# A decoder trunk on one core: both activation parts against one weight load, halves added at the eviction

## The chip, the cores and the metric

The kernel runs on one core of one Trainium2 chip. The metric is the device time of one execution in microseconds (us). Three runs of the kernel before are shown; beside them stands one profiled execution, from which every duration below is read.

## The reference

Two layers act on 256 tokens of 1024 features, in float32. Each layer is a token mixer (differential attention, block attention and latent attention side by side, merged by gates) and then a squared-ReLU MLP, each with a norm ahead and a norm behind. What matters here:

```python
h = _rms_norm(x, norm_mix_pre[l])
proj = einsum('bsd,de->bse', h, w_in[l])          # holds dq, dk, dv, mq, mk, mv, latents, gates
... three attentions, gates, output projection, x = x + norm(...)
h = _rms_norm(x, norm_mlp_pre[l])
u = square(relu(einsum('bsd,df->bsf', h, w_up[l])))      # 1024 -> 4096
x = x + _rms_norm(einsum('bsf,fd->bsd', u, w_down[l]), norm_mlp_post[l])
```

## The kernel before

**Arithmetic.** Every float32 operand of a projection is split into a high and a low part of a narrower type (fp32r), and a product is the sum of three matmuls: high weights by high activations, high by low, low by high (`mm3`, lines 174 to 179). `mm_group` (line 181) runs that triple over the eight 128-row tiles of the 1024 features, so that a block of 128 output features by 256 tokens is 24 matmuls of 256 columns, accumulated in PSUM.

**Weights.** `chunk` (line 132) loads 512 KB on the SP queue into one of five raw buffers, ScalarE (ACT) copies it to the high part (line 129), VectorE (DVE) subtracts to get the low part (line 130). There are six buffers of each part. `load_f` (line 167) brings a weight slab of 256 output columns as two chunks of four row tiles each; both of its 128-column blocks use both chunks, so a chunk comes free when the second block has passed it.

**Projections concerned.** The query and key projections of the differential attention (`dqk`) and of the block attention (`mqk`) go through `qk_proj` (line 441): four slabs each and layer, two blocks to a slab. Both blocks of a slab write the two halves of one PSUM tile of 512 columns, and one DVE instruction (line 448) evicts it, times the tokens' 1/rms. The up projection (`up`, line 721) does the same for seven of its eight groups and two slabs a group; its eviction is a ReLU on ACT (line 748), a square on ACT into the high part of `u` (line 751), a square on GpSimd (POOL, line 752) and a subtraction on DVE for the low part (line 753). The group 0 of the up projection, the value projections, the gates and the rest take other paths.

**Order of the work.** The MLP runs `up(g)` and then `down(g - 1)` for each group. In the mixer, dv and dqk are projected first, then in the program come the bias and rope constants (line 470), the latents' transposes (line 473), the differential attention, the projections mv and mqk, the block attention, the latent attention and the gates. The order in which each engine's queue holds these is worked out at build time by a planner (line 837): it places instructions by their place in the program and by when its own clock says that their inputs and buffers are there. On the chip each engine then follows that order.

**Buffers that the change touches.** PSUM tiles of the projections come from `mm_tile` (line 74), a pool of two banks. Small SBUF tiles come from `prep_tile` (line 68), a pool of three buffers that serves many names, among them `cn` (two tiles of latents, line 419, read by the transposes of line 458), `oh` (the one-hot load of the attention bias, line 261), `cb`, `lamv` and `r`.

Of the kernel before, what the change touches and what calls it, by code (L numbers as in the profile page):

```python
# [29 lines left out]
            2.7524476990947733e-06, -2.3874981991411914e-08)  # L30
# First relative distance of each T5 bucket that distances 0..255 can reach.
BUCKET_START = tuple(range(17)) + (21, 27, 35, 46, 59, 77, 99, 128, 166, 216)
# [3 lines left out]
def trunk(ctx: ExitStack, tc: tile.TileContext, x, positions, rel_bias, norm_mix_pre, norm_mix_post,  # L36
# [45 lines left out]

# [1 line left out]
    # Rows of vectors that act on features once those lie on partitions.  # L84
    n_rows = 16 + 16 + 4 + 2 + 2
# [37 lines left out]

# [1 line left out]
    def split(dst_hi, dst_lo, src, quick=False):  # L125
# [6 lines left out]
    def chunk(src, nk, c, name, parts=None, spare=None, quick=False):  # L132
        """One load of weights and its two parts; `spare` is a pool that is idle now."""
        n = nk * c
        raw = raws.tile([128, 1024], F32, tag="raw", name=f"raw_{name}")
        rv = raw[:, :n].rearrange("p (k c) -> p k c", k=nk)
        nc.sync.dma_start(rv, src)
        if spare is None:
            hi = whi.tile([128, 1024], F32R, tag="hi", name=f"hi_{name}")
            lo = wlo.tile([128, 1024], F32R, tag="lo", name=f"lo_{name}")  # L140
        else:
            pool, tag = spare
            hi = pool.tile([128, 1024], F32R, tag=tag, name=f"hi_{name}")
            lo = pool.tile([128, 1024], F32R, tag=tag, name=f"lo_{name}")
        if parts is None:
            split(hi[:, :n], lo[:, :n], raw[:, :n], quick)
        else:
            at = 0
            for v in parts(raw):
                m = v.shape[1] * v.shape[2]  # L150
                o = [t[:, at:at + m].rearrange("p (a b) -> p a b", a=v.shape[1]) for t in (hi, lo)]
                split(o[0], o[1], v)
                at += m
        return [(hi[:, k * c:(k + 1) * c], lo[:, k * c:(k + 1) * c]) for k in range(nk)]
# [4 lines left out]
    def load_t(w2d, c0, c, name, kts=KT):  # L159
        """Weights that move: kts tiles of [128, c]."""  # L160
        nk = 1024 // c
        r = []
        for k0 in range(0, kts, nk):
            r += chunk(wslice(w2d, k0, nk, c0, c), nk, c, f"{name}_{k0}")
        return r

    def load_f(w2d, c0, name, kts=KT):
        """Weights that stay: two blocks of 128 columns, kts tiles each."""
        r = []
        for k0 in range(0, kts, 4):  # L170
            r += chunk(wslice(w2d, k0, 4, c0, 256), 4, 256, f"{name}_{k0}")
        return [[(h[:, b * 128:(b + 1) * 128], l[:, b * 128:(b + 1) * 128]) for h, l in r] for b in range(2)]
# [8 lines left out]
    def mm_group(ps, stats, movs):  # L181
        n = len(stats)
        for i in range(n):
            mm3(ps, stats[i], movs[i], i == 0, i == n - 1)

    def toks(act, t):
        return [(h[:, t * 128:(t + 1) * 128], l[:, t * 128:(t + 1) * 128]) for h, l in act]

# [1 line left out]
    def new_act(name):  # L190
        return [slab_r(f"{name}{p}") for p in range(4)]

    def act_views(tiles):
        return [(tiles[k // 2][:, 0, k % 2, :], tiles[k // 2][:, 1, k % 2, :]) for k in range(KT)]

# [35 lines left out]
    def post_norm(xt, ps2, wpost, eps_col):  # L231
        """x += rms_norm(ps2) * wpost"""
        parts = small_tile("pnp", 2)
        yw = slab_tile([128, D], "yw")
        def weigh(h):
            nc.vector.tensor_tensor(yw[:, h * 512:(h + 1) * 512], ps2[h][:],
                                    wpost[:, h * 512:(h + 1) * 512], op=OP.mult)
        for h in range(2):
            nc.scalar.activation(junk, ps2[h][:], AF.Square, scale=1.0 / 32.0, accum_out=parts[:, h:h + 1])
            if h == 0:  # L240
                weigh(0)
        v = small_tile("pnv", 1)
        nc.vector.tensor_scalar(v, parts[:, 0:1], parts[:, 1:2], EPS if eps_col is None else eps_col,
                                op0=OP.add, op1=OP.add)
        q = small_tile("pnq", 1)
        rpow(q, v, 1)
        weigh(1)
        for h in range(2):
            s = slice(h * 512, (h + 1) * 512)
            nc.vector.scalar_tensor_tensor(xt[:, s], yw[:, s], q[:, 0:1], xt[:, s],  # L250
                                           op0=OP.mult, op1=OP.add)

# [1 line left out]
    bias = consts.tile([128, 9, 256], F32, name="bias")  # L254
# [22 lines left out]
    def setup_rope():  # L277
# [11 lines left out]
        for t in range(2):  # L289
            for j in range(2):  # L290
                V.tensor_scalar(ang[:, t, j, :], fr, pf[:, t:t + 1], None, op0=OP.mult)
        # Index 0: sine.  Index 1: cosine, the sine a quarter turn on.
        V.tensor_scalar(k[:, :, 0, :], ang[:, :, 0, :], 1.0 / math.pi, MAGIC, op0=OP.mult, op1=OP.add)
# [23 lines left out]
    def setup_lam():  # L317
# [10 lines left out]
        for l in range(DEPTH):  # L328
            li = 0.8 - 0.6 * math.exp(-0.3 * l)
            nc.vector.tensor_scalar(lam[:, l:l + 1], dots[:, 2 * l:2 * l + 1], dots[:, 2 * l + 1:2 * l + 2], li,  # L330
                                    op0=OP.subtract, op1=OP.add)
            # The weights come out of the chip negated: the sign goes here.
            nc.vector.tensor_scalar(subc[:, l:l + 1], cols[:, 38 + l:39 + l], -(1.0 - li), None, op0=OP.mult)

# [1 line left out]
    last_exp = [None]  # L336
# [35 lines left out]
    def av_f(ps, pt, v0, v1):  # L372
        """ps [c, 256 queries] = v^T p^T"""
        nc.tensor.matmul(ps, v0, pt[:, 0:256], start=True, stop=False)
        nc.tensor.matmul(ps[:, 128:256], v1, pt[:, 256:384], start=False, stop=True)

# [1 line left out]
    def load_c(l, k1, n):  # L378
# [5 lines left out]
    def mixer(l, xs, tiles, wc, before):  # L384
# [6 lines left out]

        # latent queries, keys and the shared rope key, token-major
        wc = wc or load_c(l, 0, 4)
# [30 lines left out]

        # 1/rms of every token along the free axis, on all partitions
        prb = tr_tile("prb")
# [14 lines left out]
        def qk_proj(off_q, off_k, p, scale, name):  # L441
            r = slab_tile([128, 2, 2, 256], f"{name}{p}")
            for j, off in ((0, off_q), (1, off_k)):
                w = load_f(win, off + p * 256, f"{name}{l}{p}{j}")
                ps = mm_tile(f"p{name}")
                for b in range(2):
                    mm_group(ps[:, b * 256:(b + 1) * 256], w[b], act)
                nc.vector.scalar_tensor_tensor(r[:, j], ps.rearrange("p (b s) -> p b s", b=2),
                                               scale if j == 0 else 1.0, rb2, op0=OP.mult, op1=OP.mult)
            return r  # L450

        # transposed latents
        def latents():
# [20 lines left out]

        # differential attention
        o_a = []
# [44 lines left out]

        # block attention: one block holds the whole sequence, so each query sees its own block
        mv = v_proj(OFF['mv'], "mv")
# [14 lines left out]

        # latent attention
        uq = []  # L540
# [85 lines left out]

        # gates and the products of the three branches, two feature blocks at a time
        branches = [[(o[j // 2][:, 0, j % 2, :], o[j // 2][:, 1, j % 2, :]) for j in range(4)] for o in (o_a, o_b, o_c)]
# [32 lines left out]

        # output projection
        wpost = load_post(norm_mix_post, l, sig_after)
# [14 lines left out]
    def finish(accs, held, xs, wpost, eps_cols, nxt, wcol, stored=None):  # L678
        """The last rows of a projection, the first half of the tokens ahead, and the norm that follows."""
        for t in range(2):  # L680
# [14 lines left out]
    def out_proj(l, w2d, act, wpost, xs):  # L695
        """x += rms_norm(mixed @ w_out); the next block's input follows each half of the tokens."""
        tiles = new_act("h2")
# [14 lines left out]
    def mlp(l, xs, tiles, before):  # L712
# [8 lines left out]
        def up(g):  # L721
# [20 lines left out]
            for p in range(2):  # L742
                w = load_f(wu, g * 512 + p * 256, f"up{l}{g}{p}")
                ps = mm_tile("pu")
                for j in range(2):
                    mm_group(ps[:, j * 256:(j + 1) * 256], w[j], act)
                r = prep_tile("r")
                nc.scalar.activation(r, ps[:], AF.Relu)
                rv = r.rearrange("p (b s) -> p b s", b=2)
                hi, lo = us[g][p][:, 0], us[g][p][:, 1]  # L750
                nc.scalar.activation(hi, rv, AF.Square)  # L751
                nc.gpsimd.tensor_tensor(r, r, r, op=OP.mult)  # L752
                nc.vector.tensor_tensor(lo, rv, hi.bitcast(F32), op=OP.subtract)
# [87 lines left out]
```

## Time and profile before

| what | value |
|---|---|
| runs, median (lowest to highest) | 875.62 us (873.63 to 876.04) |
| profiled execution, first to last instruction | 874.3 us |
| instructions | 14960, of these 5820 matmuls and as many weight loads |
| share of the span busy: TensorE (PE), DVE, ACT, POOL | 98%, 62%, 54%, 12% |
| DMA | 154.27 MB, mean 176 GB/s |
| TensorE's granted clock, mean | 0.997 of 2.4 GHz |

The page gives no time of the profiled execution but its span; the median of the runs stands 1.3 us above that. A matmul's listed duration overlaps with its neighbours' (a group of 256-column matmuls shows 283 ns each), so what a matmul costs in a full stream is read from the distance of the starts, not from the duration.

### The profile page before, as it was taken

What the parts mean: (1) busy time and instruction counts of PE and PEld (TensorE: products, weight loads), DVE (VectorE), ACT (ScalarE), POOL (GpSimd) and SP (SyncE); (2) the same over time, 40 slices, a digit from 0 to 9 for tenths busy, and PEclk for the clock granted to TensorE, in tenths of its full rate; (3) what the DMA queues carried; (4) which work ended last, traced back from release to release, by engine and by line L of the source; (5) the groups of instructions that cost most, each with busy time, mean ns of one, the idle gap of its engine ahead of it and who ended that gap; (6) DMA issues with size and microseconds to landing.
All of it is one profiled execution on the core that took longest, in us unless ns stands there. A gap on an engine that the chain in (4) does not pass through costs nothing.

```text
span 874.3 us, 14960 instructions
## 1 busy us (share of the span) xinstructions
PE 858.1 (98%) x5820; PEld 791.0 (90%) x5820; DVE 539.6 (62%) x921; ACT 468.9 (54%) x820; POOL 107.1 (12%) x130
## 2 busy tenths in 40 slices
PE   7999999999999999999999999999999999999997
PEld 6988999899988999999899899999998899999995
DVE  6757688457867445446575768954578754554452
ACT  6536675644546444445464757664544664444441
POOL 2211210001311000000100012000033010000010
PEclk9999999999999999999999999999999999999999
DMA  8865544356666656667738553546558466665631
GB/s 275 260 168 180 144 124 134 107 178 184 203 232 195 185 182 189 191 193 212 228 97 248 146 149 97 150 117 189 177 187 270 145 218 191 192 193 182 186 115 49
DMA packets 109798, 154.27 MB, mean 176 GB/s; under 512 B 5103, under 2 KB 89136, under 8 KB 109728
## 3 DMA queue, kind: packets, MB, share of 16 engines
q1 hardware_dynamic: 108448, 149.70, 56.4%
q10 hardware_dynamic: 608, 2.11, 0.7%
q0 software_dynamic: 672, 1.51, 0.6%
q8 instruction: 46, 0.75, 0.4%
q14 instruction: 24, 0.20, 0.1%
HBM read 151.19 MB, written 2.11 MB: 175 GB/s over the span
## 4 chain that ended last, share of the span: by engine, by line
PE 88%; issue 4%; DMA 3%; DVE 2%; ACT 1%; POOL 1%; SPq 0%; POOLq 0%; DVEq 0%; ACTq 0%
PE pu L176 7%; PE pu L178 7%; PE pu L177 7%; PE pd L177 6%; PE pd L178 6%; PE pd L176 6%; PE pg L176 5%; PE pg L177 5%; PE pg L178 5%; PE pb L178 3%; PE pb L177 3%; PE pb L176 3%; PE pmqk L178 2%; PE pmqk L177 2%; PE pmqk L176 2%
## 5 line engine op out<-in xcount | busy, mean ns | idle before, releaser
L177 PE MATMUL pu<-h,hi_up 128*128 128x256 f32 x448 | 126.9, 283 | 0.0
L178 PE MATMUL pu<-h,lo_up 128*128 128x256 f32 x448 | 126.8, 283 | 0.0
L176 PE MATMUL pu<-h,hi_up 128*128 128x256 f32 x448 | 126.7, 283 | 0.0
L130 DVE TENSOR_TENSOR lo_wd<-raw_wd,hi_wd 128x1024 fp32r<-128x1024 f32 x64 | 77.7, 1225 | 74.5 <-ACT hi_wd L129 74.5
L129 ACT ACTIVATE hi_wd<-raw_wd 128x1024 fp32r<-128x1024 f32 x64 | 67.0, 1058 | 82.6 <-PE pu L177 38.0
L176 PE MATMUL pg<-h,hi_g 128*128 128x256 f32 x384 | 110.6, 288 | 0.4 <-ACT lqk L602 0.4
L178 PE MATMUL pg<-h,lo_g 128*128 128x256 f32 x384 | 109.7, 286 | 0.0
L177 PE MATMUL pg<-h,hi_g 128*128 128x256 f32 x384 | 109.1, 284 | 0.0
L130 DVE TENSOR_TENSOR lo_up<-raw_up,hi_up 128x1024 fp32r<-128x1024 f32 x64 | 80.2, 1258 | 38.8 <-ACT hi_up L129 38.5
L129 ACT ACTIVATE hi_up<-raw_up 128x1024 fp32r<-128x1024 f32 x64 | 67.9, 1064 | 59.5 <-PE pu L177 29.0
L176 PE MATMUL pd<-hi_wd,u 128*128 128x512 f32 x256 | 99.9, 390 | 0.0
L177 PE MATMUL pd<-lo_wd,u 128*128 128x512 f32 x256 | 99.8, 390 | 0.0
L178 PE MATMUL pd<-hi_wd,u 128*128 128x512 f32 x256 | 99.6, 389 | 0.0
L176 PEld LDWEIGHTS pu<-h,hi_up 128*128 128x128 f32 x448 | 85.9, 192 | 0.6
L177 PEld LDWEIGHTS pu<-h,hi_up 128*128 128x128 f32 x448 | 85.9, 192 | 0.5
L178 PEld LDWEIGHTS pu<-h,lo_up 128*128 128x128 f32 x448 | 85.9, 192 | 0.1
L130 DVE TENSOR_TENSOR lo_g<-raw_g,hi_g 128x1024 fp32r<-128x1024 f32 x48 | 58.6, 1222 | 39.0 <-ACT hi_g L129 38.7
L176 PEld LDWEIGHTS pg<-h,hi_g 128*128 128x128 f32 x384 | 73.5, 191 | 1.4 <-ACT lqk L602 0.6
L177 PEld LDWEIGHTS pg<-h,hi_g 128*128 128x128 f32 x384 | 73.5, 191 | 0.5 <-issue 0.3
L178 PEld LDWEIGHTS pg<-h,lo_g 128*128 128x128 f32 x384 | 73.5, 191 | 0.1
L129 ACT ACTIVATE hi_g<-raw_g 128x1024 fp32r<-128x1024 f32 x48 | 50.5, 1057 | 40.2 <-PE pg L177 32.2
L752 POOL TENSOR_TENSOR r<-r 128x512 f32<-128x512 f32 x28 | 30.6, 1094 | 262.1 <-ACT u L751 230.9
(293 smaller groups left out, 2109.2 us busy)
## 6 DMA issues: line engine op xcount, KB each, us to landing
raw_up<-in_w_up_dram SPq DMA_DIRECT2D x64, 512.0 KB, 3.9
raw_wd<-in_w_down_dram SPq DMA_DIRECT2D x64, 512.0 KB, 4.2
raw_g<-in_w_in_dram SPq DMA_DIRECT2D x48, 512.0 KB, 3.8
raw_br<-in_w_branch_dram SPq DMA_DIRECT2D x24, 512.0 KB, 4.1
raw_dqk<-in_w_in_dram SPq DMA_DIRECT2D x16, 512.0 KB, 5.2
raw_mqk<-in_w_in_dram SPq DMA_DIRECT2D x16, 512.0 KB, 4.1
raw_wo<-in_w_out_dram SPq DMA_DIRECT2D x16, 512.0 KB, 3.9
raw_dv<-in_w_in_dram SPq DMA_DIRECT2D x8, 512.0 KB, 4.9
```

The source lines that it names most:

```text
L129: nc.scalar.activation(dst_hi, src, AF.Copy)
L130: nc.vector.tensor_tensor(dst_lo, src, dst_hi.bitcast(F32), op=OP.subtract)
L176: i = nc.tensor.matmul(ps, sh, mh, start=first, stop=False)
L177: nc.tensor.matmul(ps, sh, ml, start=False, stop=False)
L178: nc.tensor.matmul(ps, sl, mh, start=False, stop=last)
L752: nc.gpsimd.tensor_tensor(r, r, r, op=OP.mult)
```

## The change

`mm_wide` takes the place of `mm_group` in `qk_proj` and in `up` for the groups 1 to 7. The high and the low part of the activations, which lie in one tile, are passed in one matmul of 512 columns against the high weights: the high part goes to the first 256 columns of a PSUM bank, the low part to the second. The low weights by the high activations are accumulated on the first 256 columns. A block of 128 features so takes a whole PSUM tile, and `add_wide` evicts it: ACT copies the second half to SBUF, DVE adds the first half to it. In `qk_proj` the sum goes to a new tile `sum` of the prep pool, and the multiplication by 1/rms reads that. In `up` the ReLU and the square become one DVE instruction in place, ACT copies the result to the high part, and POOL's square is gone. The comment lines that the diff removes as well are left out here.

```diff
     def mm_group(ps, stats, movs):
         n = len(stats)
         for i in range(n):
-            mm3(ps, stats[i], movs[i], i == 0, i == n - 1)
+            mm3(ps, stats[i][:2], movs[i][:2], i == 0, i == n - 1)
+
+    def mm_wide(ps, stats, movs):
+        n = len(stats)
+        main = ps[:, 0:256]
+        for i in range(n):
+            (sh, sl), (mh, _, mhl) = stats[i], movs[i]
+            nc.tensor.matmul(ps.rearrange("p (b s) -> p b s", b=2), sh, mhl, start=i == 0, stop=False)
+            nc.tensor.matmul(main, sl, mh, start=False, stop=i == n - 1)
+
+    def add_wide(o, ps):
+        nc.scalar.activation(o, ps[:, 256:512], AF.Copy)
+        nc.vector.tensor_tensor(o, ps[:, 0:256], o, op=OP.add)
...
+    def both(tile, b):
+        return tile[:, 0, b, :], tile[:, 1, b, :], tile[:, :, b, :]
...
     def act_views(tiles):
-        return [(tiles[k // 2][:, 0, k % 2, :], tiles[k // 2][:, 1, k % 2, :]) for k in range(KT)]
+        return [both(tiles[k // 2], k % 2) for k in range(KT)]
...
                 w = load_f(win, off + p * 256, f"{name}{l}{p}{j}")
-                ps = mm_tile(f"p{name}")
+                s = prep_tile("sum")
                 for b in range(2):
-                    mm_group(ps[:, b * 256:(b + 1) * 256], w[b], act)
-                nc.vector.scalar_tensor_tensor(r[:, j], ps.rearrange("p (b s) -> p b s", b=2),
+                    ps = mm_tile(f"p{name}")
+                    mm_wide(ps, w[b], act)
+                    add_wide(s[:, b * 256:(b + 1) * 256], ps)
+                nc.vector.scalar_tensor_tensor(r[:, j], s.rearrange("p (b s) -> p b s", b=2),
...
                 w = load_f(wu, g * 512 + p * 256, f"up{l}{g}{p}")
-                ps = mm_tile("pu")
+                r = prep_tile("r")
                 for j in range(2):
-                    mm_group(ps[:, j * 256:(j + 1) * 256], w[j], act)
-                r = prep_tile("r")
-                nc.scalar.activation(r, ps[:], AF.Relu)
+                    ps = mm_tile("pu")
+                    mm_wide(ps, w[j], act)
+                    add_wide(r[:, j * 256:(j + 1) * 256], ps)
+                nc.vector.scalar_tensor_tensor(r, r, 0.0, r, op0=OP.max, op1=OP.mult)
                 rv = r.rearrange("p (b s) -> p b s", b=2)
                 hi, lo = us[g][p][:, 0], us[g][p][:, 1]
-                nc.scalar.activation(hi, rv, AF.Square)
-                nc.gpsimd.tensor_tensor(r, r, r, op=OP.mult)
+                nc.scalar.activation(hi, rv, AF.Copy)
                 nc.vector.tensor_tensor(lo, rv, hi.bitcast(F32), op=OP.subtract)
```

## Rows read from the trace of the kernel before

**Rows 1.** The page: busy us, share of the span, instructions of each engine.
```profile
PE 858.1 (98%) x5820; PEld 791.0 (90%) x5820; DVE 539.6 (62%) x921; ACT 468.9 (54%) x820; POOL 107.1 (12%) x130
```

**Rows 2.** The page: the chain that ended last, share of the span by engine.
```profile
PE 88%; issue 4%; DMA 3%; DVE 2%; ACT 1%; POOL 1%; SPq 0%; POOLq 0%; DVEq 0%; ACTq 0%
```

**Rows 3.** Groups by line and shape: line, engine, names, shapes, count, busy, mean, idle before.
```profile
L177 PE MATMUL pu<-h,hi_up 128*128 128x256 f32 x448 | 126.9, 283 | 0.0
L177 PE MATMUL pmqk<-h,hi_mqk 128*128 128x256 f32 x128 | 37.6, 294 | 0.0
L177 PE MATMUL pdqk<-h,hi_dqk 128*128 128x256 f32 x128 | 36.2, 283 | 0.0
```

**Rows 4.** Timeline of PE: start us, us, what. One stream of each width, first and last.
```profile
296.53 0.28 PE L176 MATMUL pu<-h,hi_up 128*128 128x256 f32 x1
...
302.29 0.28 PE L176 MATMUL pu<-h,hi_up 128*128 128x256 f32 x1
...
399.79 0.39 PE L176 MATMUL pd<-hi_wd,u 128*128 128x512 f32 x1
...
408.41 0.39 PE L178 MATMUL pd<-hi_wd,u 128*128 128x512 f32 x1
```

**Rows 5.** Groups by line and shape: evictions and elementwise steps, before or nearest to the new ones.
```profile
L752 POOL TENSOR_TENSOR r<-r 128x512 f32<-128x512 f32 x28 | 30.6, 1094 | 262.1 <-ACT u L751 230.9 <-DVE lo_wd L130 31.2
L751 ACT ACTIVATE u<-r 128x512 fp32r<-128x512 f32 x28 | 17.7, 632 | 0.8
L748 ACT ACTIVATE r<-pu 128x512 f32<-128x512 f32 x28 | 16.2, 579 | 2.5 <-PE pu L178 2.5
L250 DVE SCALAR_TENSOR_TENSOR x<-yw,pnq,x 128x512 f32<-128x512 f32 x16 | 11.3, 749 | 0.4
L448 DVE SCALAR_TENSOR_TENSOR dqk<-pdqk,rb 128x512 f32<-128x512 f32 x8 | 5.5, 684 | 0.0
L670 DVE TENSOR_TENSOR ob<-sc,ob 128x256 fp32r<-128x256 f32 x8 | 3.3, 418 | 0.1
L669 ACT ACTIVATE ob<-sc 128x256 fp32r<-128x256 f32 x8 | 3.1, 383 | 2.5 <-PE sc L375 2.4
```

**Rows 6.** Timeline of ACT and DVE behind the block boundary at 302.29.
```profile
302.37 1.06 ACT L129 ACTIVATE hi_wd<-raw_wd 128x1024 fp32r<-128x1024 f32 x1 [0.38 <-PE pu L177]
...
303.33 0.58 ACT L748 ACTIVATE r<-pu 128x512 f32<-128x512 f32 x1
...
303.46 1.23 DVE L130 TENSOR_TENSOR lo_wd<-raw_wd,hi_wd 128x1024 fp32r<-128x1024 f32 x1 [0.22 <-ACT hi_wd L129]
```

**Rows 7.** Timeline: PE stopped by DVE, and its first two matmuls after that.
```profile
267.28 0.29 DVE L211 CAST h<-xt 128x256 fp32r<-128x256 f32 x1 [1.60 <-ACT xt L205]
...
267.63 0.50 PE L176 MATMUL pu<-hi_up,h 128*128 128x512 f32 x1 [0.61 <-DVE h L211]
...
267.96 0.40 PE L177 MATMUL pu<-lo_up,h 128*128 128x512 f32 x1
```

**Rows 8.** Busy time by engine in the first layer's differential attention; PEclk, DMA share, GB/s last.
```profile
69.00:104.00 35.00, 33.02 (x247) 30.88 (x246) 25.47 (x72) 22.46 (x65) 4.96 (x14) 0.95 0.50 143
```

**Rows 9.** Timeline of POOL: the last early load, and the one-hot load.
```profile
5.47 0.57 POOL L281 DMA_DIRECT2D freq<-in_inv_freq_dram  x1
...
26.27 0.56 POOL L262 DMA_DIRECT2D oh<-in_onehot_dram  x1
```

**Rows 10.** The chain that ended last, in order of time: the way of the attention bias.
```profile
26.27 5.44 DMA oh<-in_onehot_dram
...
62.94 6.38 DMA bias<-scr
69.35 0.29 DVE e L345
```

**Rows 11.** Timeline of PE: the one long stop in the first layer's attention.
```profile
73.57 0.33 PE L361 MATMUL ppt<-ident,e 128*128 128x128 f32 x1 [1.98 <-DVE e L495]
```

More of the change, by code (lines that the diff above doesn't have):

```diff
@@ L183, in mm_group @@
         for i in range(n):
-            mm3(ps, stats[i], movs[i], i == 0, i == n - 1)
+            mm3(ps, stats[i][:2], movs[i][:2], i == 0, i == n - 1)
[9 more added lines that the diff above has]
+        nc.vector.tensor_tensor(o, ps[:, 0:256], o, op=OP.add)
     def toks(act, t):
-        return [(h[:, t * 128:(t + 1) * 128], l[:, t * 128:(t + 1) * 128]) for h, l in act]
+        return [(a[0][:, t * 128:(t + 1) * 128], a[1][:, t * 128:(t + 1) * 128]) for a in act]
+    def both(tile, b):
+        return tile[:, 0, b, :], tile[:, 1, b, :], tile[:, :, b, :]
     def new_act(name):
```

## The prediction

> **What bounds the kernel now.** First the page's shares: PE is busy 98% of the span, no other engine above 62% [rows 1]. A listed busy share of PE overstates, since matmuls overlap, so the second view is the chain of waits: 88% of the end's chain runs over PE, 4% over issue, 3% over DMA [rows 2]. Third, the groups by line: in the three projections that change, the 448 + 128 + 128 instructions of line 177 (one for each triple) show no idle time of PE before them [rows 3]. So PE's stream sets the time, and a matmul taken out of it is worth its distance in the stream, as long as the eviction still clears the two PSUM banks in time. The fourth view, the timeline of PE, gives the distances: 48 matmuls of 256 columns lie between the starts 296.53 and 302.29, 5.76 / 48 = 0.120 us each; 38 distances of 512 columns between 399.79 and 408.41, 8.62 / 38 = 0.2268 us each [rows 4]. Twice the columns thus cost 0.2268 and not 0.240: each matmul carries about 13 ns that don't grow with its columns.
>
> **PE, part by part.** 448 + 256 = 704 triples of 3 x 0.120 = 0.360 become a 512-column and a 256-column matmul, 0.2268 + 0.120 = 0.3468 us. Gain 0.0132 x 704 = 9.3 us, all on the path. As many weight loads go; they lie beside the matmuls already. The trace has no matmul whose moving operand comes in two pieces of 256 columns, 512 apart, as the new wide one does. Bounds: nothing extra (as the 512-column rows), or the price of two matmuls of 256, 0.240, which leaves a gain of 0. I take nothing extra, the nearest row in columns.
>
> By the Trainium skill's page "TensorE: Matmul & The Clock Gate", section "Back-to-back issue gap", an isolated warm matmul takes N / 2.4 ns plus 2.5. By that a triple would save 2.5 ns, 1.8 us in all, an estimate from that page of the Trainium skill. The rows at full clock show 13 ns for the same term, and the measurement decides; by the page's figure the change could not pay for what follows.
>
> **The eviction.** A block now fills a bank of its own, and lasts 8 x 0.3468 = 2.77 us. With two banks, the block after the next may start only when ACT's copy and DVE's addition are through. The first block of a slab meets idle engines: copy 0.38 and addition 0.42, by the nearest forms of 256 columns that read PSUM [rows 5], some 1.0 us with hand-offs; 1.8 us to spare. The second block ends just as the slab's last weight chunk comes free, and the planner puts the next weight split ahead of the eviction. With the boundary at 302.29 [rows 4], ACT starts that split at +0.08 (released by line 177, which precedes the block's last matmul), the eviction only at +1.04, and DVE starts the low part at +1.17, for 1.23 [rows 6]. In the new kernel the copy then ends at +1.04 + 0.38 = +1.42, but DVE is with the low part until +2.40, and the addition ends at +2.82. The bank is wanted at +2.77. DVE's end to PE's start took 0.06 (267.57 to 267.63), and the stopped matmul's successor came after 0.33 in place of 0.227 [rows 7]: so 0.11 us late and 0.10 to pick up, about 0.2 us for each such hand-over, at worst. It hangs on a few hundredths. There are 14 in the up projection (one for each group: the second slab's second block wants the bank of the first slab's second) and 12 within the four runs of q/k slabs. Before, a slab had 5.76 us for this and the pair of banks never ran short. Bounds: 0 (the planner puts a ready matmul of the down projection in the gap) and 26 x 0.2 = 5.2 us. I take half, 2.5 us.
>
> **ACT, DVE, POOL.** Up, each of 28 slabs: ACT loses 0.58 + 0.63 and gains 2 x 0.38 and a copy of 512 columns, 0.63 like the square; DVE gains 2 x 0.42 and the ReLU-square, 0.75 by the nearest form with two SBUF operands; POOL loses 1.09 [rows 5]. DVE's 28 x 1.6 = 45 us lie beside PE: it stands at 62%. The path from a slab to `u` is not on the critical one, since down(g) follows a whole up and down later; if that cover went, it would cost the difference of the chains, about 0.3 us. In q/k each of 16 slabs adds 0.77 on ACT and 0.84 on DVE, and the scaling reads SBUF: 0.75 for 0.68. In dqk this meets little else. In the mqk run of the first layer, beside the differential attention, DVE has 25.5 of 35 us, ACT 22.5 [rows 8]; eight blocks add 3.4 + 0.3 and 3.1. DVE at 83% still leaves room, but the softmax steps that PE waits for lie in the same queues. Bounds 0 and 3.4 us a layer (all of DVE's share on the path); I take 0.5 a layer, 1 in all, nearer the lower end since PE has projections to run meanwhile.
>
> **Buffers of the prep pool.** Three buffers; in dqk two are held by `cn`. In the first layer `oh` took the third: POOL was done with early loads at 6.04, yet issued `oh` only at 26.27 [rows 9], while loads that stand later in the program (freq) had long gone. This speaks for buffers handed out in program order. Four tiles `sum` now stand ahead of `oh`. If so, its load moves behind dqk, and the bias, which is first used at 69.35 now, comes later by the load's 5.44 and 0.56 of issue, 6 us [rows 9, 10]; PE has mv and mqk to run until then. What it costs is decided by how well the planner's clock knows these loads: now PE stops 1.98 us for it at 73.57 [rows 11], and a mean clock of 0.95 over 35 us [rows 8] means 3.5 us at the half level (1.2 of 2.4 GHz) behind that stop, 1.75 us lost; 3.7 together. If `oh` keeps its place, the first `sum` waits until PE has passed the bias matmul or the transposes of `cn`, about 1 us, and the bias comes earlier: the 3.7 may go. Bounds -3.7 and +3.7; I take 0.
>
> **Sum.** -9.3 + 2.5 + 1 = -5.8 us. Against the profiled execution 874.3 becomes 868.5 of span; the runs lie 1.3 above it by their median, so 875.6 becomes 869.8, rounded to 870.
>
> **Rivals.**
> 1. Full gain: hand-overs fit, and the stop of the first layer goes: -9.3 - 3.7 + 1 = -12.0, and with half of the stop -10: 863.6 to 866. For: the hand-over misses by hundredths only. Against: the three loads on the way to the bias remain, the last alone 6.38 us [rows 10].
> 2. The gain is eaten: 5.2 at the hand-overs, 3 around the attention: 874.5. For: the order of split and eviction [rows 6] is the planner's habit. Against: PE has other ready work in the up stage.
> 3. The fixed cost does not go with the matmul: if most of the 13 ns belongs to the change of weights between two slabs of columns and returns behind the wide one, say 2 of the 9.3 us stay: -2 + 3.5 = +1.5, 877.1. Against: the 13 ns stand at both widths [rows 4]. The Trainium skill's page above would put the saving here.
> 4. The wide matmul runs as two pieces: 0 + 3.5 = 879.1. That the change doesn't save what it says. No row for or against.
> 5. Slower by the banks: the addition stands behind one more low part, 1.23 us more at each hand-over. At 14 of them: 14 x 1.3 = 18.6, less 9.3: 885; at all 26, 900. It decides from 9.3 / 26 = 0.36 us for each hand-over. For: DVE is in order and its low parts come in rows of two and three where loads are late. Against: after the second block of a slab just one split is free to run.
>
> **How the numbers follow.** Chances: forecast 0.50 (own range 867 to 873), rival 1 0.17, rival 2 0.15, rival 3 0.03, rival 4 0.07, rival 5 0.08. A measurement of this kernel tells about 0.3%, 2.6 us, from no change: faster is under 873.0, slower over 878.2. Faster: 0.50 + 0.17 + 0.02 of rival 2 = 0.69; same: 0.13 + 0.03 = 0.16; slower: 0.07 + 0.08 = 0.15. The range goes from 864.5 (inside rival 1) to 878.0, which leaves out rivals 4 and 5 and the edge of rival 1.
>
> **What would show it.** Right: 704 fewer matmuls; wide matmuls 0.227 apart; an up block 2.77 us long; at the second slab's second block a stop of PE of at most 0.2 us that names DVE. Wrong: wide matmuls 0.240 apart (rival 4); stops of 1 us and over at these places with DVE on a low part (rival 5); PE's granted clock at the half level in the up stage; in the first layer, a stop of more than 4 us before the first transposes of the attention's weights, with the one-hot load issued only after dqk.

## The result and the profile after

The changed kernel takes 884.77 us (median of 4 runs, 884.11 to 885.55), the kernel before 875.12 beside it: ratio 1.0116 [1.0101, 1.013], 9.65 us slower where 5.8 faster was forecast. The profiled execution took 884.64, with a span of 882.9 against 874.3.

The page of the changed kernel, first its engines and its chain [rows 1, 2], then the two instructions that took the place of the changed triples [rows 3]:

```profile
PE 857.2 (97%) x5116; PEld 752.7 (85%) x5116; DVE 590.1 (67%) x1037; ACT 482.7 (55%) x880; POOL 78.7 (9%) x102
...
PE 92%; DMA 2%; ACT 2%; issue 1%; DVE 1%; POOL 0%; SPq 0%; DVEq 0%; POOLq 0%; ACTq 0%
...
L193 PE MATMUL pu<-h,hi_up 128*128 128x512 f32 x448 | 159.3, 396 | 0.0
...
L194 PE MATMUL pu<-h,lo_up 128*128 128x256 f32 x448 | 125.6, 280 | 0.0
```

The 704 matmuls are gone, and neither new group shows idle time before it. So the loss isn't a wait at the changed instructions of the up projection. The view of PE's waits of the changed kernel (who waits for whom; us in total, times, the longest) shows where part of it is:

```profile
PE ppt L379 <- DVE e L515: 4.1, 1, 4.1
PE pcols L113 <- DMA rows<-in_norm_mix_pre_dram: 3.3, 1, 3.3
PE pmqk L193 <- ACT mv L456: 2.7, 1, 2.7
PE pin L219 <- DMA x<-in_x_dram: 2.6, 2, 2.3
PE pin L219 <- DVE x L268: 1.7, 1, 1.7
PE sc L520 <- ACT pt L381: 1.7, 2, 1.5
```

Before, the waits at `pmqk`, `sc` and `pin` on DVE were not among PE's listed waits, and the one at `ppt` was 1.98 [rows 11]. Of the longer ones three (`ppt`, `pmqk`, `sc`) lie in the first layer's attention; together they take 8.3 us, where before there was one of 1.98. PE's timeline there, in the changed kernel:

```profile
72.19 0.79 PE L193 MATMUL pmqk<-h,hi_mqk 128*128 128x512 f32 x1 [2.75 <-ACT mv L456]
...
86.29 0.48 PE L379 MATMUL ppt<-ident,e 128*128 128x128 f32 x1 [4.08 <-DVE e L515]
...
88.86 0.58 PE L520 MATMUL sc<-dv,pt 128*128 128x128 f32 x1 [1.49 <-ACT pt L381]
...
448.35 0.44 PE L219 MATMUL pin<-ident,x 128*128 128x128 f32 x2 [1.66 <-DVE x L268]
```

`ppt` waits for the exponentials, these for the bias. Its way begins on POOL's timeline, which answers to [rows 9]; the two transfers behind it are from the chain [rows 10], the first use from DVE's timeline:

```profile
5.24 0.57 POOL L299 DMA_DIRECT2D freq<-in_inv_freq_dram  x1
60.45 0.56 POOL L280 DMA_DIRECT2D oh<-in_onehot_dram  x1 [34.87 <-DVE dqk L468]
69.13 0.53 POOL L290 DMA_DIRECT2D scr<-cb  x1 [0.46 <-DVE cq L484]
73.94 1.04 POOL L292 DMA_DIRECT2D bias<-scr  x1 [4.28 <-DMA scr<-cb]
```

```profile
69.13 4.52 DMA scr<-cb
73.94 8.09 DMA bias<-scr
```

```profile
82.06 0.29 DVE L363 CUSTOM_DVE_ANT_0 e<-sc,bias 128x128 f32<-128x128 f32 x1 [4.52 <-DMA bias<-scr]
```

POOL stands 34.87 us at the one-hot load, until the last scaling of `dqk` frees the buffer: 60.45 against 26.27 before. The bias comes into use at 82.06 against 69.35 [rows 10]. The same stretch of windows as [rows 8] (columns as there):

```profile
69.00:104.00 35.00, 26.68 (x133) 21.82 (x134) 19.78 (x63) 17.98 (x54) 5.63 (x12) 0.85 0.49 143
```

PE works 26.68 of 35 us in place of 33.02, and its mean granted clock is 0.85: behind the stops it runs part of the time at 1.2 instead of 2.4 GHz. What of the loss goes to the lower clock and what to smaller stops was not told apart.

By stages (us between the first matmuls of the stages, from the starts in the traces; E1, E12 and E10 are experiments below: no tile `sum`; the kernel before with the bias set up first; E1 with the matmuls grouped by width):

| stage | before | after | E1 | E12 | E10 |
|---|---|---|---|---|---|
| first mixer, to the first `pu` | 260.5 | 269.9 | 256.9 | 254.6 | 255.4 |
| first MLP | 182.3 | 183.1 | 183.0 | 182.3 | 179.8 |
| second mixer | 243.7 | 243.5 | 244.9 | 243.7 | 243.1 |
| second MLP, to the end | 187.8 | 186.4 | 186.4 | 187.8 | 185.2 |

The whole loss (9.4) is in the first mixer; the MLPs, where 64% of the triples are, give back 0.6 together, where the forecast's gain for their 448 triples was 448 x 0.0132 = 5.9.

### The profile page after: what moved, and what is told of

The parts are those of the page before. It is cut to its first block, busy times and chain, and to the rows that moved or that the text cites. A ratio compares the mean times of both kernels' runs of the same rounds, so it can differ in the third digit from the quotient of the medians.

```text
span 882.9 us, 13655 instructions
## 1 busy us (share of the span) xinstructions
PE 857.2 (97%) x5116; PEld 752.7 (85%) x5116; DVE 590.1 (67%) x1037; ACT 482.7 (55%) x880; POOL 78.7 (9%) x102
## 4 chain that ended last, share of the span: by engine, by line
PE 92%; DMA 2%; ACT 2%; issue 1%; DVE 1%; POOL 0%; SPq 0%; DVEq 0%; POOLq 0%; ACTq 0%
PE pu L193 12%; PE pd L176 6%; PE pd L177 6%; PE pd L178 6%; PE pu L194 6%; PE pg L176 5%; PE pg L178 5%; PE pg L177 5%; PE pdqk L193 4%; PE pb L178 3%; PE pb L177 3%; PE pb L176 3%; PE pmqk L193 2%; PE pdqk L194 2%; PE sc L373 2%; PE po L176 2%
## 5 line engine op out<-in xcount | busy, mean ns | idle before, releaser
L193 PE MATMUL pu<-h,hi_up 128*128 128x512 f32 x448 | 159.3, 396 | 0.0
L193 PEld LDWEIGHTS pu<-h,hi_up 128*128 128x128 f32 x448 | 84.1, 188 | 20.1
L176 PEld LDWEIGHTS pd<-hi_wd,u 128*128 128x128 f32 x256 | 47.9, 188 | 10.3
L178 PEld LDWEIGHTS pd<-hi_wd,u 128*128 128x128 f32 x256 | 47.8, 188 | 10.0
L177 PEld LDWEIGHTS pd<-lo_wd,u 128*128 128x128 f32 x256 | 48.1, 188 | 9.4
```

The source lines that it names most:

```text
L176: i = nc.tensor.matmul(ps, sh, mh, start=first, stop=False)
L177: nc.tensor.matmul(ps, sh, ml, start=False, stop=False)
L178: nc.tensor.matmul(ps, sl, mh, start=False, stop=last)
L193: nc.tensor.matmul(ps.rearrange("p (b s) -> p b s", b=2), sh, mhl, start=i == 0, stop=False)
```

## The experiments

Two theories. A: the extra tile `sum` pushes the one-hot load behind `dqk`, and the late bias costs about 11 us in the first layer. B: the time goes where I had priced load and hand-overs (ACT and DVE beside attention, two PSUM banks), and the tile is harmless. Ratios are to the kernel before, run on the same chip, with 95% intervals.

**E1, no tile `sum`.** The halves are added into the result tile and scaled in place; matmuls and evictions stay.

```diff
-                s = prep_tile("sum")
...
-                    add_wide(s[:, b * 256:(b + 1) * 256], ps)
-                nc.vector.scalar_tensor_tensor(r[:, j], s.rearrange("p (b s) -> p b s", b=2),
+                    add_wide(r[:, j, b, :], ps)
+                nc.vector.scalar_tensor_tensor(r[:, j], r[:, j],
```

> Theory A (the sums' tiles in the prep pool hold back the one-hot load, and with it the attention bias of the first layer): without tile `sum` the load is issued near 26 us again, the bias is used near 70 us or earlier, the stops of PE at 72, 86 and 89 us (9.5 us together) go, and the time falls from 884.8 to 873-876 us. Rival B (the two-step eviction loads ACT and DVE beside the softmax and slows the attention): every copy and addition is still there, so the time stays at 882-885.

873.29 against 874.59: 0.999 [0.9972, 1.0008]. POOL's and DVE's timelines of E1:

```profile
24.78 0.56 POOL L280 DMA_DIRECT2D oh<-in_onehot_dram  x1
...
40.30 1.04 POOL L292 DMA_DIRECT2D bias<-scr  x1 [3.50 <-DMA scr<-cb]
```

```profile
52.23 0.28 DVE L363 CUSTOM_DVE_ANT_0 e<-sc,bias 128x128 f32<-128x128 f32 x1
```

The bias is used 30 us earlier than after and 17 earlier than before. Against each one's own run of before, the tile alone costs 9.65 + 1.30 = 11.0 us, give or take 2 by the two intervals. A holds. But the forecast's gain isn't there either, although the bias is now earlier than before: E1's interval takes in no change at all.

**E2, the late load alone, in the kernel before.** A one-element tile, written from the last result of `dqk`, takes the third prep buffer ahead of the one-hot load.

```diff
+            hold = prep_tile("hold")
+            nc.vector.tensor_copy(hold[:, 0:1], dqk[1][:, 1, 1, 255:256])
```

> The kernel before, with one tile of the prep pool more, written by a one-column copy after the last dqk eviction and placed ahead of the one-hot load. Theory A: the load moves from 26 us to about 56-60 us, the bias is used 6 to 12 us later than 69 us, PE stops in the first layer's attention, time 881-886 us against 875.1. Rival B: nothing of the eviction has changed, 875 us.

879.53 against 874.59: 1.0054 [1.0034, 1.0074], 4.9 us, under the expected 6 to 11. POOL's timeline shows the same delay as after, DVE's the same late use, and PE stops near two of the same times, the second time at another instruction (the profiled execution was the longest of the five, 882.68 us):

```profile
59.38 0.56 POOL L262 DMA_DIRECT2D oh<-in_onehot_dram  x1 [33.62 <-DVE hold L471]
```

```profile
81.60 0.29 DVE L345 CUSTOM_DVE_ANT_0 e<-sc,bias 128x128 f32<-128x128 f32 x1 [5.93 <-DMA bias<-scr]
```

```profile
72.00 0.39 PE L176 MATMUL pmqk<-h,hi_mqk 128*128 128x256 f32 x1 [1.70 <-ACT mv L438]
...
85.70 0.38 PE L176 MATMUL pmqk<-h,hi_mqk 128*128 128x256 f32 x1 [1.92 <-DVE mqk L448]
```

The late load by itself makes a kernel slower whose matmuls are untouched.

**E3 and E4, each half of the change alone.** E3 has the up projection new and query/key as before; E4 the reverse. Core of E3:

```diff
-                    mm_wide(ps, w[b], act)
-                    add_wide(s[:, b * 256:(b + 1) * 256], ps)
+                    mm_group(ps[:, b * 256:(b + 1) * 256], w[b], act)
```

> The changed kernel with the query and key projections as before; wide matmuls in the up projection alone. Theory A: no tile `sum`, the first layer as before; both MLPs together gave 0.6 us in the trace of the changed kernel (0.8 lost in the first, 1.4 won in the second), so 874.5 us, 873 to 876. Rival B expects the same; a time over 880 would say that the loss lies in the MLP and speak against both.

> The changed kernel with the up projection as before; wide matmuls in the query and key projections alone. Theory A and rival B: all of the loss is here, 885 us, 883 to 887. If the two halves don't add up to the whole within 2 us, the planner's order couples them.

E3: 873.42 against 874.59, 0.9986 [0.9965, 1.0006]. E4: 886.43, 1.0123 [1.01, 1.0145]. Both within what A expects, and the two halves add up to the whole within 2 us (-1.2 + 11.8 = 10.7 against 9.65). The loss sits in the query and key projections, which bring the tile; the up projection, with 448 of the triples, gives 1.2 us in the medians, which the interval doesn't tell from nothing.

**E5, why the pair is dearer.** Start to start, a wide and a narrow matmul take 234.4 + 116.7 = 351.1 ns in after and in E1 (means over the 448 pairs of the up projection), not 346.8. E5 is E1 with the two parts of each activation block side by side, so that the wide operand is one piece of 512 columns.

```diff
-            nc.tensor.matmul(ps.rearrange("p (b s) -> p b s", b=2), sh, mhl, start=i == 0, stop=False)
+            nc.tensor.matmul(ps[:], sh, mhl, start=i == 0, stop=False)
...
-        return tile[:, 0, b, :], tile[:, 1, b, :], tile[:, :, b, :]
+        return tile[:, b, 0, :], tile[:, b, 1, :], tile[:, b].rearrange("p a s -> p (a s)")
```

> As e1 (sum made in place), and the high and low part of each activation block lie side by side, so that the wide matmul's moving operand is one piece of 512 columns. If the two pieces are what makes a wide matmul 0.233 us in place of 0.227: 0.227 in the stream, 704 x 6 ns = 4 us less than e1, 869-870 us. If it is the change between matmuls of 512 and 256 columns: still 0.233 and the time of e1, 873 us.

874.06 against 874.83: 0.9994 [0.9985, 1.0004]; the pair keeps 234.4 + 116.7. The two pieces cost nothing, so the change between widths is left to test (E10).

**E6, three banks for projections** (one for transposes), on E1, and **E8**, the same on E5.

```diff
-    p_mm = ctx.enter_context(tc.tile_pool(name="pmm", bufs=2, space=PSUM))
-    p_tr = ctx.enter_context(tc.tile_pool(name="ptr", bufs=2, space=PSUM))
+    p_mm = ctx.enter_context(tc.tile_pool(name="pmm", bufs=3, space=PSUM))
+    p_tr = ctx.enter_context(tc.tile_pool(name="ptr", bufs=1, space=PSUM))
```

> As e1, with three PSUM banks for the projections and one for the transposes. If the late hand-over of a bank is why the planner puts down matmuls between the up blocks and so delays the last group: up and down are whole again, the stop of 1.8 us at the end of the first MLP is gone, 870.5-872 us. If one bank for the transposes costs more in the attention than that, 874 us and more, with PE's stops at transposes there.

> Both edits of e5 and e6: if both effects are real and independent, 867-869 us, below the kernel before by 0.7% and over; if neither is, 873.

E6: 876.61 against 874.83, 1.0017 [1.0006, 1.0028]; E8: 876.2, 1.0017 [1.0009, 1.0026]. E6 lies where its second branch put it, though not by stops at the attention's transposes; E8 misses both of its own. In after and E1 the order in the up stage had become 32 matmuls of `pu`, 9 of `pd`, 16, 7, 16, 32, where before whole groups of 96 and 48 took turns; with three banks most groups are whole again (64 and 48), and the stop at the MLP's end is gone. But PE now stops elsewhere, at the starts of stages, where it waits for `h`; I put that down to the single transpose bank. PE's waits in E6:

```profile
PE pu L176 <- DVE h L229: 4.6, 4, 1.2
...
PE pc L176 <- DVE h L229: 1.2, 1, 1.2
PE pc L178 <- DVE h L230: 1.2, 1, 1.2
```

Before, `pu` waited 1.2 in two stops. So this pair doesn't price the banks; E9 does it without that side effect.

**E9, four banks in the up projection alone,** on E1: the second block of a slab takes a transpose bank.

```diff
-                    ps = mm_tile("pu")
+                    ps = mm_tile("pu") if j == 0 else tr_tile("pu")
```

> As e1 (sum made in place), and in the up projection a slab's second block takes one of the two transpose banks, which are idle there; the transposes keep their two banks. If the late hand-over of a bank makes the planner split up and down: up and down whole, no stop of 1.8 us at the end of the first MLP, no stops at the transposes as in e6, 869.5-871.5 us. If not: 873 us as e1.

871.69 against 874.28: 0.9968 [0.9957, 0.9979], 0.2 above the expected range. From the third group on the order is whole, and `pin` at the first MLP's end starts without the 1.66 of wait. Over E1 that is 1.3 us in the medians, too little for the two intervals to tell from nothing.

**E10, the matmuls grouped by width,** on E1: the eight wide ones of a block, then its eight narrow ones.

```diff
             nc.tensor.matmul(ps.rearrange("p (b s) -> p b s", b=2), sh, mhl, start=i == 0, stop=False)
+        for i in range(n):
+            (sh, sl), (mh, _, mhl) = stats[i], movs[i]
             nc.tensor.matmul(main, sl, mh, start=False, stop=i == n - 1)
```

> As e1, but a block's eight wide matmuls come first and its eight narrow ones behind them. If the change of width is what makes a pair 0.350 us in place of 0.347: 14 of 16 changes a block go, a pair takes 0.347, some 2 us less. The slab's high parts also come free 0.9 us before the block's end, so that the weight split no longer stands ahead of the eviction: 869-872 us. If the change of width is not it: a pair still 0.350, and only the hand-over gains, 871-873 us.

864.62 against 874.28: 0.9889 [0.9873, 0.9906], 9.7 us faster than before and better than either branch. PE's timeline, one block of E1 (its first pair and last narrow one, and the matmul behind it), then one of E10:

```profile
300.44 0.39 PE L193 MATMUL pu<-h,hi_up 128*128 128x512 f32 x1
300.66 0.28 PE L194 MATMUL pu<-h,lo_up 128*128 128x256 f32 x1
...
303.13 0.28 PE L194 MATMUL pu<-h,lo_up 128*128 128x256 f32 x1
303.25 0.40 PE L176 MATMUL pd<-hi_wd,u 128*128 128x512 f32 x1
```

```profile
298.45 1.98 PE L193 MATMUL pu<-h,hi_up 128*128 128x512 f32 x8
300.26 1.11 PE L196 MATMUL pu<-h,lo_up 128*128 128x256 f32 x8
301.21 0.40 PE L178 MATMUL pd<-hi_wd,u 128*128 128x512 f32 x1
```

E1: (303.25 - 300.44) / 8 = 0.351 us for a pair. E10: (300.26 - 298.45) / 8 = 0.226 and (301.21 - 300.26) / 8 = 0.119; the means over all pairs of the up projection are 227.8 + 118.9 = 346.7 ns, the forecast's figure. A change between high and low weights alone doesn't cost this: the triples before make it too, at 0.120 a matmul [rows 4]. The pitch gives 704 x 0.0044 = 3.1 of the 8.4 us that E10 gains on E1. PE's waits of E1, then of E10, show more:

```profile
...
PE pqn L176 <- ACT lqk L621: 2.2, 2, 1.1
PE pin L219 <- DVE x L268: 1.7, 1, 1.7
PE pin L219 <- DMA x<-in_x_dram: 1.6, 1, 1.6
PE pu L176 <- DVE h L229: 1.2, 2, 0.6
PE pdqk L193 <- DVE dqk L199: 0.7, 1, 0.7
```

```profile
...
PE pin L221 <- DMA x<-in_x_dram: 2.2, 2, 1.3
PE pu L176 <- DVE h L231: 1.2, 2, 0.6
PE sc L394 <- ACT pt L383: 0.8, 2, 0.4
```

The waits at `pqn`, `dqk` and the first MLP's end, 4.6 us together, are gone. The high halves of a slab's second block are read some 0.95 us before the block ends, and I take it that the split that waits for them then runs ahead of the eviction; no run moved the split alone.

**E11, grouped and four banks.**

> Both edits of e9 and e10. If both effects hold: 867.5-870 us, under the kernel before by 0.5% and over. If the change of width is not it: as e9.

864.28 against 874.28: 0.9889 [0.9874, 0.9905], below the expected range and the same as E10. With grouped matmuls two more banks in the up projection bring nothing.

**E12, the bias first, in the kernel before.** `setup_bias` is called ahead of `dqk`, with no other edit, to see how much of E10 is due to the bias alone.

```diff
-        dqk = [qk_proj(OFF['dq'], OFF['dk'], p, 0.125, "dqk") for p in range(2)]
         if l == 0:
             setup_bias()
+        dqk = [qk_proj(OFF['dq'], OFF['dk'], p, 0.125, "dqk") for p in range(2)]
```

> The kernel before with the bias set up ahead of the dqk projections in the program, nothing else. In e1 and e10 PE passes the bias matmul near 34 us, in the kernel before near 55 us, and PE's stop at 73.6 us is gone there. If that early bias is worth a stop and its slow clock: 871.5-873 us, so that of the 10 us of e10 some 2 to 3 are not the matmuls'. If it is worth nothing: 874-875 us, and all 10 us belong to the matmuls and their order.

870.7 against 874.45: 0.9953 [0.9939, 0.9968]. The bias is used at 59.12, and the stop of [rows 11] is gone. 3.75 us, more than expected (the range ended at 871.5). If the early bias is worth as much in E10, the matmuls' part of its 9.7 is 5.9.

**E13, grouped, but with the tile `sum`.**

> The changed kernel with the wide matmuls of a block ahead of its narrow ones, and tile `sum` in the prep pool as in the change. If the late one-hot load and the order of the matmuls are two separate causes, the load still goes out near 60 us and the time is that of e10 plus what e1 took off the changed kernel, 864.6 + 11.5 = 876 us, 874 to 878. If the grouping frees the eviction and with it the pool, under 870 us.

876.58 against 874.45: 1.0024 [1.0015, 1.0033], as expected. On POOL's timeline the load is late again:

```profile
60.08 0.56 POOL L282 DMA_DIRECT2D oh<-in_onehot_dram  x1 [33.43 <-DVE dqk L470]
```

Late load and order of the matmuls are separate causes: the tile costs 11.0 us with pairs and 2.13 + 9.66 = 11.8 grouped; grouping gives 9.65 - 2.13 = 7.5 with the tile and 9.66 - 1.30 = 8.4 without.

## Why the prediction was wrong

| term of the sum, us | forecast | measured | from |
|---|---|---|---|
| PE's stream, 704 triples | -9.3 | -6.3 | 704 x (0.3600 - 0.3511) |
| hand-overs, and ACT and DVE beside attention | +2.5 + 1 | +8.75 | E1 less E12 (-1.30 + 3.75 = +2.45), without the -6.3 |
| buffers of the prep pool | 0 | +7.2 | tile 11.0 less the 3.75 that E12 gets from an early bias |
| sum | -5.8 | +9.65 | |

The pitch of 0.3511 is that of the up projection's pairs, and the row below it holds what is left. By the intervals of the runs that row and the next are known to about 2 us each.

**"Buffers of the prep pool", the step that turned the sign.** Its reading was right: buffers go in program order, the load moves behind `dqk`, the bias comes later. What failed is "I take 0" between the bounds of -3.7 and +3.7. An early bias gives 3.75 (E12), as the lower bound has it. The upper one was taken from the wait that was already there [rows 11], with a new delay of 6 us. The delay is 12.7 (82.06 - 69.35): the load came 34 us later, and the two transfers behind it waited anew, for DVE and for the transfer ahead. And "PE has mv and mqk to run until then" covers too little: PE ran the three blocks of `mqk` that stood ahead of `ppt` in its fixed order, and then stopped for 4.08 us. The next block comes only at 90.17. It had no free bank either, for the two copies that empty the banks stand on ACT behind exponentials that waited for the bias:

```profile
87.31 0.36 ACT L198 ACTIVATE sum<-pmqk 128x256 f32<-128x256 f32 x1
...
88.07 0.37 ACT L198 ACTIVATE sum<-pmqk 128x256 f32<-128x256 f32 x1
```

E2 shows 4.9 of the 7.2 with the old matmuls, and there `ppt` never waits more than 0.6 for DVE. The other 2.3 are within the noise of these differences; if they are real, this stop, which E2 doesn't have, is the likely place, but no run moved it alone.

**The gain of PE.** The term per triple was right for a stream of one width: grouped, the up projection's pair takes 346.7 ns against 346.8 forecast, by which all 704 would gain 704 x 0.0133 = 9.4 us. The change alternates widths, and that costs 4.4 ns for each pair, 3.1 us. I had asked only whether the wide operand's two pieces cost something; E5 says no. The rows of [rows 4] were streams of equal matmuls, and a mixed stream was not priced. In `dqk` the change gained nothing at all: by PE's starts the first layer's 192 matmuls took 23.12 us before (31.90 to 55.02), the 128 that took their place 17.18 + 3.02 + 2.93 = 23.13. Part of that is the hand-over that the prediction worked out. PE's timeline and DVE's, where a block wants its bank:

```profile
45.05 0.50 PE L193 MATMUL pdqk<-h,hi_dqk 128*128 128x512 f32 x1
45.39 0.28 PE L194 MATMUL pdqk<-h,lo_dqk 128*128 128x256 f32 x1
```

```profile
43.44 1.23 DVE L130 TENSOR_TENSOR lo_mv<-raw_mv,hi_mv 128x1024 fp32r<-128x1024 f32 x1 [0.16 <-ACT hi_mv L129]
44.58 0.42 DVE L199 TENSOR_TENSOR sum<-pdqk,sum 128x256 f32<-128x256 f32 x1
```

The addition stands behind a low part and ends at 45.00, PE starts at 45.05, and the successor comes 0.34 later in place of 0.234. Eight of the 128 wide matmuls of `dqk` in after stand 0.31 to 0.34 ahead of their successor; whether each of them is this hand-over is not shown. In the table this loss is in the row of the hand-overs.

The page "TensorE: Matmul & The Clock Gate" of the Trainium skill, section "Back-to-back issue gap", gives an isolated matmul 2.5 ns beside its columns, by which a triple would save 2.5 ns (an estimate from that page of the Trainium skill); it says itself that a stream of weight loads and matmuls is spaced otherwise. The runs show 8.9 ns alternated and 13.3 grouped, so for these streams the measurement decides, and the isolated figure is not to be carried over.

**Hand-overs and the elementwise load.** The timing at the boundary came as worked out. ACT's timeline of E1, then DVE's, where an up block ends at 298.37:

```profile
298.50 1.06 ACT L129 ACTIVATE hi_wd<-raw_wd 128x1024 fp32r<-128x1024 f32 x1 [0.36 <-PE pu L193]
299.47 0.36 ACT L198 ACTIVATE r<-pu 128x256 f32<-128x256 f32 x1
```

```profile
299.60 1.23 DVE L130 TENSOR_TENSOR lo_wd<-raw_wd,hi_wd 128x1024 fp32r<-128x1024 f32 x1 [0.19 <-ACT hi_wd L129]
300.74 0.42 DVE L199 TENSOR_TENSOR r<-pu,r 128x256 f32<-128x256 f32 x1
```

The split goes ahead of the copy and the low part ahead of the addition, as [rows 6] foretold. The copy starts 0.97 behind the split (forecast 0.96), the addition 1.14 behind the low part (1.23). In the up stage PE doesn't wait there: the planner fills the gap with 9 or 7 matmuls of `pd`. That is the lower bound's mechanism, and still the first MLP ends with a wait of 1.66 on DVE. The split order alone isn't shown to cause it: it is gone with the whole order of E9, but also in E10, whose order is split as much (32, 8, 16, 6, 16, 34). From the stages, E1 against E12 loses 2.7 and 0.6 in the two MLPs beside the gain of 2.0 each, and 3.5 and 2.4 in the mixers beside 1.15 each. By these spans that is 9.1 where the medians give 8.75. With grouping (E10 against E12, the grouped gain taken off) 0.4 and 0.4 are left in the MLPs, 2.5 and 1.1 in the mixers. So, grouped, the up stage costs 0.8 where its 14 of the 26 hand-overs were forecast at 1.3; the mixers cost 3.6 where their 12 hand-overs and the load beside attention were forecast at 1.2 + 1. Which of these two it is was not separated.

**The rivals.** Rival 1 (full gain) would have needed the early bias and grouping. Rival 2, the eaten gain, is E1 less the bias effect: +2.45 against its -1.1, dearer than it said. Rival 3 (the fixed cost returns) is refuted grouped, where the 13 ns go as far as forecast; alternated, 4.4 of them return. Rival 4 is refuted by the pitch (234.4 and not 240) and by E5. Rival 5 didn't come: slower, but not by the banks, whose price in the up stage is about 1.3 us (E9). (Its 14 x 1.3 is 18.2 and not 18.6, which changes nothing.) The sign that I had named for the way it went, a stop over 4 us before the first transposes with the one-hot load behind `dqk`, stands in the trace (4.08); it had no chance of its own.

Without the two faults, tile and alternation, the sum comes out near the forecast: E10 is 9.66 us faster than before, and without the 3.75 of an early bias 5.9, against 5.8. That is in part luck, for the up stage cost less and the mixers more than forecast. For a kernel to keep, E10 is it.

## What to carry to other kernels

A new tile in a shared pool is a place in a queue: list what is handed the pool's buffers behind it in program order, follow each to the first instruction of the bounding engine that needs it, and price the delay there as a stop; adding into the result tile avoids it. When matmuls of two widths belong to one sum, run each width in a row: here the pitch was 4.4 ns a pair shorter, and one half of the weights is done with earlier. A pitch read from a stream of equal instructions is not that of a mixed one.

## What was not expected of the hardware

A 512-column matmul followed by a 256-column one, each with its own weights, took 234.4 + 116.7 ns in turns, and 227.8 + 118.9 in rows of eight, with the same data (E1 and E10, from start to start). A moving operand in two pieces of 256 columns, 512 apart, took as long as one piece (234.4 in both). One transfer of 1152 KB, `bias<-scr`, took 6.38 us before (from 62.94), 8.09 after (73.94), 8.0 in E1 (40.30) and 9.8 in E12 (38.86), so being late is not what lengthens it. Why alternation costs time, and why this transfer differs, is open.
